# Four-layer decoder trunk on one core: VectorE's work on a finished set dealt out over the next set's steps, the last set's columns ended in two halves

## The chip, the cores and the metric

The kernel runs on one core of a Trainium2 chip. The metric is the device time of one execution in microseconds (us), the median of the runs shown. Engines are named as the profile names them: PE (TensorE, matmuls), PEld (its weight loads), DVE (VectorE), ACT (ScalarE), POOL (GpSimd) and SP (SyncE, which here issues the weight transfers).

## What is computed

The reference runs a trunk of depth 2 over 256 positions of width 2048, in float32. Layer 0 mixes with a recurrent head group and a pooling mixer, layer 1 with sparse attention. Each layer then runs an MLP and a gated embedding add, and a final norm closes:

```
hn = rmsnorm(h, ln_mix_g[i]);  h = h + mixer(hn)                       # w_in, w_out
hn = rmsnorm(h, ln_mlp_g[i]);  h = h + square(relu(hn @ w_up)) @ w_down   # 2048 -> 8192 -> 2048
gate = sigmoid(rmsnorm(h, ln_ple_g[i]) @ ple_w_gate[i])                # 2048 -> 2048
h = h + gate * (p[i] @ ple_w_proj[i])                                  # 256 -> 2048
return rmsnorm(h, ln_final_g)
```

## The kernel before, in words

**Products in three terms.** Every float32 weight is split as it arrives: ScalarE copies it to a rounded high part (`emit_hi`, L203), VectorE subtracts that from the weight and so makes the low part (`emit_lo`, L210). Activations are split in the same way. A product is three matmuls: high by high, low by high, high by low (`product`, L703 to L705). Only the third needs VectorE's low part.

**Steps and lookahead.** A list `steps` holds one entry for each half of a 1 MB weight load (two blocks of 128 rows by 512 columns). `run` goes through it: it emits the high parts up to two steps ahead, the step's matmuls (12 in a plain step), then what `after(n, fn)` put off to this step, and last the low part of the step two ahead. There are four buffers each for high and low parts, and three for raw loads. Each engine executes its own instructions strictly in the order in which they are emitted, so this order is the schedule.

**Sets.** The projections of 2048 output columns are done in two sets of 1024 columns (`mm_set`, index `n2`). A set accumulates over its steps into four PSUM banks, two 128-row halves of the positions (t) by two 512-column halves (n); the next set uses the other four. Two of the eight weight loads of an MLP set go through extra sums that save matmuls ("own" steps, `SUM_PAIRS`); their results come out in two side tiles `w`, made by `out1` to `out3` near the end of the set.

**The end of a set.** When the last matmul of a set is emitted, `post` puts the set's remaining work on the list. For a set of the MLP's down projection (`h_out`, 16 of them) VectorE does `wide` twice (L809, 1024 columns: the side tiles into h) and `adds` twice (L816, two instructions of 512 columns each: the banks into h); all of it is emitted with the set's last step, ahead of the low part of the step two later. Only the last two down sets of a layer (q = 3) also call `x_after`, which transposes the new h on TensorE (L787), splits it into the next input X, and squares it for the norm. The output projections of the mixers use the same `h_out`, without side tiles. The sets of the gate (`gate`, four of them) run a tanh on ScalarE (L998) and two VectorE instructions per 512-column piece (L1003, L1004), eight in all, again with the set's last step. In layer 1 the squares of the final norm (L1028) follow, and after the last set `finish` makes the reciprocal root, scales h in four pieces of 1024 columns (L1036) and sends them out (L1037). The small projection `proj` of the embedding is put between steps of each gate set.

Of the kernel before, what the change touches and what calls it, by code (L numbers as in the profile page):

```python
# [9 lines left out]
F32 = mybir.dt.float32  # L10
# [102 lines left out]
def trunk(ctx: ExitStack, tc: tile.TileContext, a: dict, out: bass.AP):  # L113
# [81 lines left out]
    def emit_hi(s):  # L195
        u, k0, nk = halves[s]["at"]
        dmas(u + AHEAD - 1)
        w = loads[u]["w"]
        if "add" not in halves[s]:
            halves[s]["src"] = loads[u]["raw"][:, k0:k0 + nk, :w]  # L200
        halves[s]["hi"] = hip.tile([P, 2, 512], F32R, name="hi")
        for k in (slice(0, 1), slice(1, nk)) if s == 0 else (slice(0, nk),):
            act.activation(halves[s]["hi"][:, k, :w], halves[s]["src"][:, k, :], AF.Copy)  # L203
# [33 lines left out]
    def after(n, fn):  # L237

        later.setdefault(state["step"] + n, []).append(fn)
# [440 lines left out]
    def wtiles():  # L680
        return utile().rearrange("p a b -> p (a b)").rearrange("p (n c) -> p n c", c=512), ph["w2"]

    def mm_set(src, order, X, post, own=(), S=None, between={}, hooks={}):


        B, n_set = ph["B"], ph["sets"]
# [80 lines left out]
        def out3():  # L767
            w1, w2 = w["w"]
            dve.scalar_tensor_tensor(w2[:, 1], w2[:, 0], -1.0, w2[:, 1], op0=OP.mult, op1=OP.subtract)

        for i, p in enumerate(order):
            if i in between:
                between[i]()
            if i in hooks:
                add_hook(hooks[i])
            parts = own_fns(p) if p in own else [(0, 2, None, plain(p, 0)), (2, 2, None, plain(p, 1))]
            add_blocks(src(p), parts)
# [21 lines left out]
    def h_out(n2, r, X, gi, sx=None, w_first=True):  # L799

        def post(w, banks):
            hb = lambda t, n: h[:, t, n2 * 1024 + n * 512:n2 * 1024 + (n + 1) * 512]

            def wide(t):
                ht = h[:, t, n2 * 1024:(n2 + 1) * 1024].rearrange("p (n c) -> p n c", c=512)
                if r is None:
                    dve.tensor_tensor(ht, ht, w[t], op=OP.add)
                else:
                    dve.scalar_tensor_tensor(ht, w[t], r[:, t:t + 1], ht, op0=OP.mult, op1=OP.add)  # L809

            def adds(n):
                for t in range(2):
                    if r is None:
                        dve.tensor_tensor(hb(t, n), hb(t, n), banks[t][n], op=OP.add)
                    else:
                        dve.scalar_tensor_tensor(hb(t, n), banks[t][n], r[:, t:t + 1], hb(t, n), op0=OP.mult, op1=OP.add)  # L816
            if w is not None:
                after(0, lambda: (wide(0), wide(1)))
            after(0, lambda: adds(0))
            after(0, lambda: adds(1))  # L820
            if X is not None:
                x_after(n2, banks, X, gi, sx)
        return post

    def x_after(n2, banks, X, gi, sx=None, at=0):
# [74 lines left out]
    def mlp(l, X, Xn):  # L900
# [3 lines left out]
        def up_out(q, n2):  # L904
            def post(w, banks):
                W = w or wtiles()

                def adds(n):
                    for t in range(2):
                        if w:  # L910
                            dve.tensor_tensor(W[t][:, n], banks[t][n], W[t][:, n], op=OP.add)  # L911

                def relu(n):
                    for t in range(2):
                        act.activation(W[t][:, n], W[t][:, n] if w else banks[t][n], AF.Relu)  # L915
                    for t in range(2):
                        act.activation(W[t][:, n], W[t][:, n], AF.Square)

                def back(n):
                    for i in (2 * n, 2 * n + 1):  # L920
                        turn(banks, i, lambda t, n, c: W[t][:, n, c * P:(c + 1) * P])

                def high(i):
                    k = 2 * i
                    act.activation(Hs[n2][:, k:k + 2, :T], scratch(banks, i), AF.Copy)  # L925

                def low(i):
                    k = 2 * i
                    dve.tensor_tensor(Hs[n2][:, k:k + 2, T:], scratch(banks, i), Hs[n2][:, k:k + 2, :T].bitcast(F32),  # L929
                                      op=OP.subtract)  # L930

                def sums():
                    v = [W[t][:, 1].rearrange("p (i j c) -> p i j c", j=2, c=P) for t in range(2)]
                    s_sums(v[0][:, :, 0], v[0][:, :, 1], v[1][:, :, 0], v[1][:, :, 1])

                def s_back(i):
                    b = scratch(banks, i).rearrange("p j (s n) -> p (j s) n", n=P)
                    for o in range(4):
                        pe.transpose(b[:, o], ph["f"][:, i, o], ident)

                def s_split(i):
                    b = scratch(banks, i).rearrange("p j (s n) -> p (j s) n", n=P)
                    S = ph["S"][1][:, i]
                    act.activation(S[:, :, :P], b, AF.Copy)
                    dve.tensor_tensor(S[:, :, P:], b, S[:, :, :P].bitcast(F32), op=OP.subtract)
                for n in range(2):
                    after(n, lambda n=n: (adds(n), relu(n)))
                    after(1 + n, lambda n=n: back(n))
                    for i in (2 * n, 2 * n + 1):
                        after(2 + n, lambda i=i: high(i))  # L950
                        after(2 + n, lambda i=i: low(i))
                if n2 == 0:
                    after(3, sums)
                    for i in range(2):
                        after(4, lambda i=i: s_back(i))
                        after(5, lambda i=i: s_split(i))
            return post

        Hs = []
# [16 lines left out]
    def ple(l, X, Xn):  # L976
# [11 lines left out]
            ph["sets"] = n_set  # L988

        def gate(n2):  # L990
            def post(w, banks):
                W = wtiles()
                at = 0
                hb = lambda t, n: h[:, t, n2 * 1024 + n * 512:n2 * 1024 + (n + 1) * 512]

                def tanh(n):
                    for t in range(2):
                        act.activation(W[t][:, n], banks[t][n], AF.Tanh, scale=HALF[:, t:t + 1])  # L998

                def add(n):  # L1000
                    for t in range(2):
                        e = st["e"][:, t, n2 * 1024 + n * 512:n2 * 1024 + (n + 1) * 512]
                        dve.scalar_tensor_tensor(W[t][:, n], W[t][:, n], 1.0, e, op0=OP.add, op1=OP.mult)  # L1003
                        dve.tensor_tensor(hb(t, n), hb(t, n), W[t][:, n], op=OP.add)  # L1004
                for n in range(2):
                    after(at, lambda n=n: tanh(n))
                    after(at, lambda n=n: add(n))
                if l == 0:
                    x_after(n2, banks, Xn, G_MIX + 16, at=at)
                    if n2 == 1:  # L1010
                        after(at + 4, rstd_of)
                else:
                    for n in range(2):
                        after(at, lambda n=n: last_squares(n2, n))
                    if n2 == 1:
                        after(at, finish)
            return post

        def load_e():
            st["e"] = big(F32, (P, 2, D))  # L1020
            if l == 1:
                st["g"] = big(F32, (P, 2, D))[:, 0]
                g = a["gfin"]
                nc.scalar.dma_start(st["g"], g.to_broadcast([P, D]))

        def last_squares(n2, n):
            for t in range(2):
                act.activation(jk, h[:, t, n2 * 1024 + n * 512:n2 * 1024 + (n + 1) * 512], AF.Square,  # L1028
                               accum_out=ssq[:, t, 2 * n2 + n:2 * n2 + n + 1])

        def finish():
            rstd_of()
            for t in range(2):
                for n2 in range(2):
                    c = slice(n2 * 1024, (n2 + 1) * 1024)
                    dve.scalar_tensor_tensor(h[:, t, c], h[:, t, c], RSTD[:, t:t + 1], st["g"][:, c], op0=OP.mult, op1=OP.mult)  # L1036
                    (nc.sync if n2 == 0 else nc.scalar).dma_start(out[:, t, c], h[:, t, c])  # L1037

        add_hook(load_e)
        for n2 in range(2):  # L1040
            mm_set(lambda p, n2=n2: a["ple_w_gate"][l][n2][p], range(8), X, gate(n2), between={5: lambda n2=n2: proj(n2)},
                   hooks={5: rstd_of} if n2 == 0 else {})
        add_hook(ph["close"])

    X1 = new_x()
# [340 lines left out]
```

## Time and profile before

| | us |
|---|---|
| median of 3 runs | 2342.57 (2340.16 to 2343.86) |
| the profiled execution, its own time | 2343.47 |
| its span, first to last instruction | 2341.4 |
| TensorE busy | 2283.6 (98%) |
| VectorE busy | 1738.2 (74%) |
| ScalarE busy | 1314.3 (56%) |
| mean granted TensorE clock | 0.995 |

How to read it: TensorE is busy nearly all of the span, and its matmuls overlap in the pipeline, so one of 512 columns is listed with 390 ns though the next starts 227 ns behind it. What can be won without changing the matmuls lies in the places where TensorE waits, in stretches at a lower clock, and behind the last matmul. The list of waits gives the first, the windows the second, the timeline the third.

### The profile page before, as it was taken

To read this page: it belongs to the slowest core of one execution; us is meant where nothing else is said; L and a number is where in the kernel's file an instruction comes from. 1 tells how busy PE (TensorE), PEld (TensorE's weight loads), DVE (VectorE), ACT (ScalarE), POOL (GpSimd) and SP (SyncE) were. 2 spreads that over 40 slices of the span, in tenths; PEclk is the share of its full clock that TensorE was granted. 3 is DMA by queue.
4 is the path that set the end of the run, shared out by engine and by line. 5 is a ranking of instruction groups with operands and counts; after the bars stand their busy time and mean duration, and the time that the engine had idled before them with its cause. 6 is when DMAs were issued, how large, how long until landed. Compare 5 with 4: busy or idle time off the path is not lost.

```text
span 2341.4 us, 30197 instructions
## 1 busy us (share of the span) xinstructions
PE 2283.6 (98%) x11510; PEld 1933.2 (83%) x11510; DVE 1738.2 (74%) x2360; ACT 1314.3 (56%) x1900; POOL 15.5 (1%) x42
## 2 busy tenths in 40 slices
PE   8999999999999999999999999999999999999997
PEld 8998887787787788888889988888788788788876
DVE  6786687788787788756875675688777877877864
ACT  6665564564465466555564554656456456455563
POOL 2000000000000000000000000000000000000000
PEclk9999999999999999999999999999999999999998
DMA  7545555555555555555775224555555555455553
GB/s 264 199 168 193 183 180 201 194 181 198 183 184 192 184 191 180 198 182 191 258 273 181 82 84 160 185 197 187 184 199 185 176 203 196 164 208 190 194 182 123
DMA packets 69264, 436.55 MB, mean 186 GB/s; under 512 B 9856, under 2 KB 14336, under 8 KB 18176
## 3 DMA queue, kind: packets, MB, share of 16 engines
q1 hardware_dynamic: 64272, 426.85, 52.2%
q10 hardware_dynamic: 4848, 7.79, 1.0%
q8 instruction: 90, 1.47, 0.3%
q14 instruction: 54, 0.44, 0.1%
HBM read 432.51 MB, written 2.10 MB: 186 GB/s over the span
## 4 chain that ended last, share of the span: by engine, by line
PE 94%; DVE 4%; issue 1%; DMA 1%; ACT 0%; SPq 0%; DVEq 0%; ACTq 0%
PE ps L705 24%; PE ps L703 24%; PE ps L704 24%; PE ps L293 10%; PE ps L297 3%; PE ps L787 2%; DVE lo L210 2%; PE ps L298 1%; PE ps L1328 1%; PE ps L1118 1%; DVE h L816 1%; DMA raw<-in_ab_w_in 1%; PE ps L1270 0%; PE ps L1268 0%; DVE h L1004 0%
## 5 line engine op out<-in xcount | busy, mean ns | idle before, releaser
L210 DVE TENSOR_TENSOR lo<-raw,hi 128x1024 fp32r<-128x1024 f32 (+1 forms) x817 | 937.9, 1166 | 228.8 <-ACT hi L203 227.2
L203 ACT ACTIVATE hi<-raw 128x1024 fp32r<-128x1024 f32 (+1 forms) x817 | 818.4, 1014 | 504.3 <-PE ps L704 396.1
L705 PE MATMUL ps<-lo,big 128*128 128x512 f32 x2496 | 976.3, 391 | 31.3 <-DVE lo L210 31.3
L703 PE MATMUL ps<-hi,big 128*128 128x512 f32 x2496 | 979.7, 393 | 0.0
L704 PE MATMUL ps<-hi,big 128*128 128x512 f32 x2496 | 973.7, 390 | 0.0
L705 PEld LDWEIGHTS ps<-lo,big 128*128 128x128 f32 x2496 | 469.9, 188 | 136.7 <-DVE lo L210 38.9
L704 PEld LDWEIGHTS ps<-hi,big 128*128 128x128 f32 x2496 | 470.4, 188 | 96.0
L703 PEld LDWEIGHTS ps<-hi,big 128*128 128x128 f32 x2496 | 470.2, 188 | 95.4
L293 PE MATMUL ps<-big,hi 128*128 128x256 f32 x1408 | 264.0, 289 | 7.2 <-ACT hi L203 7.2
L210 DVE TENSOR_TENSOR lo<-big,hi 128x1024 fp32r<-128x1024 f32 x128 | 156.6, 1223 | 136.8 <-ACT hi L203 136.8
L203 ACT ACTIVATE hi<-big 128x1024 fp32r<-128x1024 f32 x128 | 135.8, 1061 | 215.6 <-PE ps L704 201.7
L293 PEld LDWEIGHTS ps<-big,hi 128*128 128x128 f32 x1408 | 222.7, 193 | 9.2 <-ACT hi L203 7.2
L293 PE MATMUL ps<-big,lo 128*128 128x256 f32 x704 | 200.4, 285 | 2.5 <-DVE lo L210 2.5
L293 PEld LDWEIGHTS ps<-big,lo 128*128 128x128 f32 x704 | 135.6, 193 | 3.3 <-DVE lo L210 3.3
L297 PE MATMUL ps<-big,hi 128*128 128x512 f32 x320 | 113.6, 398 | 0.0
L298 PE MATMUL ps<-big,lo 128*128 128x256 f32 x320 | 89.7, 280 | 0.7 <-DVE lo L210 0.5
L734 DVE TENSOR_TENSOR big<-raw 128x1024 f32<-128x1024 f32 x64 | 78.0, 1219 | 0.2
L297 PEld LDWEIGHTS ps<-big,hi 128*128 128x128 f32 x320 | 60.1, 188 | 14.1
L929 DVE TENSOR_TENSOR big<-ps,big 128x512 fp32r<-128x512 f32 x64 | 41.1, 684 | 36.5 <-ACT big L925 36.5
L298 PEld LDWEIGHTS ps<-big,lo 128*128 128x128 f32 x320 | 60.3, 189 | 2.0 <-DVE lo L210 1.5
L409 ACT ACTIVATE big<-ps,gains 128x256 fp32r<-128x256 f32 x80 | 31.3, 474 | 49.5 <-PE ps L787 49.5
L915 ACT ACTIVATE u<-u 128x512 f32<-128x512 f32 x32 | 19.9, 623 | 55.5 <-DVE u L911 55.5
(235 smaller groups left out, 1525.2 us busy)
## 6 DMA issues: line engine op xcount, KB each, us to landing
raw<-in_mlp_w_up SPq DMA_DIRECT2D x128, 1024.0 KB, 4.9
raw<-in_mlp_w_down SPq DMA_DIRECT2D x128, 1024.0 KB, 4.9
raw<-in_c_w_in SPq DMA_DIRECT2D x36, 1024.0 KB, 4.9
raw<-in_ple_w_gate SPq DMA_DIRECT2D x32, 1024.0 KB, 4.9
raw<-in_ab_w_in SPq DMA_DIRECT2D x20, 1024.0 KB, 5.0
raw<-in_ab_w_out SPq DMA_DIRECT2D x16, 1024.0 KB, 4.9
raw<-in_c_w_out SPq DMA_DIRECT2D x16, 1024.0 KB, 4.9
raw<-in_c_cmp_w_k SPq DMA_DIRECT2D x8, 1024.0 KB, 4.9
```

Source lines behind the costliest of these rows:

```text
L203: act.activation(halves[s]["hi"][:, k, :w], halves[s]["src"][:, k, :], AF.Copy)
L210: dve.tensor_tensor(lo[:, k, :w], src[:, k, :], halves[s]["hi"][:, k, :w].bitcast(F32), op=OP.subtract)
L293: pe.matmul(b, lhsT=wt[:, kk, cols], rhs=x[:, x0:x0 + T], start=first and n == 0 and j % 2 == 0, stop=last and n == 2, skip_group_check=True)
L297: pe.matmul(b, lhsT=hi[:, kk, cols], rhs=x, start=first, stop=False, skip_group_check=True)
L298: pe.matmul(b[:, T:], lhsT=lo[:, kk, cols], rhs=x[:, :T], start=False, stop=last, skip_group_check=True)
L409: act.activation(dst[:, :T], src, AF.Copy, **kw)
L703: pe.matmul(b, lhsT=x_hi, rhs=hi[:, n, :], start=r not in begun, stop=False, skip_group_check=True)
L704: pe.matmul(b, lhsT=x_lo, rhs=hi[:, n, :], start=False, stop=False, skip_group_check=True)
L705: pe.matmul(b, lhsT=x_hi, rhs=lo[:, n, :], start=False, stop=end, skip_group_check=True)
L734: dve.tensor_tensor(t, raw[:, 0::3, :], raw[:, 1:2, :].to_broadcast([P, 2, 512]), op=OP.add)
L787: pe.transpose(b[:, j, t * P:(t + 1) * P], of(t, i // 2, (2 * i + j) % 4), ident)
L929: dve.tensor_tensor(Hs[n2][:, k:k + 2, T:], scratch(banks, i), Hs[n2][:, k:k + 2, :T].bitcast(F32), op=OP.subtract)
```

## The change

Four things are changed.

1. `h_out`: with side tiles, `wide(0)`, `wide(1)`, `adds(0)` and `adds(1)` are emitted one, two, three and four steps after the set's last step, each between two low parts; `x_after` moves with them by three steps. Without side tiles, `adds(1)` moves one step.
2. The gate's pieces: the second 512-column piece is emitted one step after the first. `proj` is put before the fifth weight load instead of the sixth. In `up_out` the sums of the side input move one step.
3. The final norm of layer 1: h times the gain vector is made piece by piece on VectorE (`hg`, two instructions per piece) for all pieces but the very last; the scale by the reciprocal root is then one factor per row.
4. The last set: the last two weight loads are used column half by column half (`column`), so that the banks of n = 0 end two steps before those of n = 1, and `last(0)` runs beside them. After the last tanh a one-element Sqrt (`warm`) brings ScalarE's function table in; `finish` scales the prepared pieces on ScalarE and VectorE and sends five pieces from SP.

```diff
@@ emit_hi
-            halves[s]["src"] = loads[u]["raw"][:, k0:k0 + nk, :w]
+            at = k0 if isinstance(k0, slice) else slice(k0, k0 + nk)
+            halves[s]["src"] = loads[u]["raw"][:, at, :w]
@@ mm_set
+        def column(p, n):
+            def fn(hi, lo):
+                for k in range(2):
+                    for t in range(2):
+                        product(PLAIN[t][n], A(p, k, t), hi, lo, k, k == 1 and p == order[-1])
+                if p == order[-1]:
+                    by_n(n, [acc_of(PLAIN[t][n]) for t in range(2)])
+            return fn
+
         for i, p in enumerate(order):
+            if by_n and i == len(order) - 2:
+                us = [len(loads), len(loads) + 1]
+                for q in order[i:]:
+                    loads.append({"src": src(q), "nk": 4, "w": 512})
+                for n in range(2):
+                    for u, q in zip(us, order[i:]):
+                        halves.append({"at": (u, slice(n, 4, 2), 2)})
+                        steps.append(("w", len(halves) - 1, column(q, n)))
+                return
@@ h_out
-            if w is not None:
-                after(0, lambda: (wide(0), wide(1)))
-            after(0, lambda: adds(0))
-            after(0, lambda: adds(1))
+            at = 0 if w is None else 3
+            for t in range(0 if w is None else 2):
+                after(1 + t, lambda t=t: wide(t))
+            for n in range(2):
+                after(at + n, lambda n=n: adds(n))
             if X is not None:
-                x_after(n2, banks, X, gi, sx)
+                x_after(n2, banks, X, gi, sx, at)
@@ up_out
-                    after(3, sums)
+                    after(4, sums)
...
@@ gate
+            def last(n, banks):
+                W = st.setdefault("W", None) or wtiles()
+                st["W"] = W if n == 0 else None
+                end = n2 == 1 and n == 1
+                for t in range(2):
+                    act.activation(W[t][:, n], banks[t], AF.Tanh, scale=HALF[:, t:t + 1])
+                if end:
+                    act.activation(warm, epsb, AF.Sqrt)
+                for t in range(2):
+                    dve.scalar_tensor_tensor(W[t][:, n], W[t][:, n], 1.0, eb(t, n), op0=OP.add, op1=OP.mult)
+                    dve.tensor_tensor(hb(t, n), hb(t, n), W[t][:, n], op=OP.add)
+                    last_square(t, n2, n)
+                for t in range(0 if end else 2):
+                    dve.tensor_tensor(hg(t, n), hb(t, n), gb(n), op=OP.mult)
+                if end:
+                    finish()
+
             def post(w, banks):
+                if l == 1:
+                    for n in range(2):
+                        after(n, lambda n=n: last(n, [banks[t][n] for t in range(2)]))
+                    return
...
                 for n in range(2):
-                    after(at, lambda n=n: tanh(n))
-                    after(at, lambda n=n: add(n))
+                    after(n, lambda n=n: tanh(n))
+                    after(n, lambda n=n: add(n))
...
         def finish():
-            rstd_of()
-            for t in range(2):
-                for n2 in range(2):
-                    c = slice(n2 * 1024, (n2 + 1) * 1024)
-                    dve.scalar_tensor_tensor(h[:, t, c], h[:, t, c], RSTD[:, t:t + 1], st["g"][:, c], op0=OP.mult, op1=OP.mult)
-                    (nc.sync if n2 == 0 else nc.scalar).dma_start(out[:, t, c], h[:, t, c])
+            mean_square()
+            act.activation(RSTD, MS, AF.Sqrt, scale=1.0 / D, bias=epsb)
+            dve.reciprocal(RSTD, RSTD)
+            o = st["hg"]
+            c = slice(1536, 2048)
+            for t in range(2):
+                r = RSTD[:, t:t + 1]
+                dve.scalar_tensor_tensor(o[:, t, c], h[:, t, c], r, st["g"][:, c], op0=OP.mult, op1=OP.mult)
+                b = slice(768 * t, 768 * t + 768)
+                act.activation(o[:, 0, b], o[:, 0, b], AF.Copy, scale=RSTD[:, 0:1])
+                nc.sync.dma_start(out[:, 0, b], o[:, 0, b])
+            nc.sync.dma_start(out[:, :, c], o[:, :, c])
+            for t in range(2):
+                b = slice(768 * t, 768 * t + 768)
+                dve.tensor_scalar(o[:, 1, b], o[:, 1, b], RSTD[:, 1:2], None, op0=OP.mult)
+                nc.sync.dma_start(out[:, 1, b], o[:, 1, b])
@@ the gate's sets
-            mm_set(lambda p, n2=n2: a["ple_w_gate"][l][n2][p], range(8), X, gate(n2), between={5: lambda n2=n2: proj(n2)},
-                   hooks={5: rstd_of} if n2 == 0 else {})
+            post, last = gate(n2)
+            mm_set(lambda p, n2=n2: a["ple_w_gate"][l][n2][p], range(8), X, post, between={4: lambda n2=n2: proj(n2)},
+                   hooks={5: rstd_of} if n2 == 0 else {}, by_n=last if l == 1 and n2 == 1 else None)
```

## Rows read from the trace of the kernel before

**Rows 1.** The page: busy us, share of the span, instructions.
```profile
PE 2283.6 (98%) x11510; PEld 1933.2 (83%) x11510; DVE 1738.2 (74%) x2360; ACT 1314.3 (56%) x1900; POOL 15.5 (1%) x42
```
**Rows 2.** Waits of PE, whole span: waiter, releaser, us in total, times, longest.
```profile
PE ps L705 <- DVE lo L210: 31.3, 18, 2.1
```
**Rows 3.** Timeline of PE, end of a down set: start, us, instruction, idle before.
```profile
434.23 0.39 PE L704 MATMUL ps<-hi,big 128*128 128x512 f32 x1
436.61 0.50 PE L705 MATMUL ps<-lo,big 128*128 128x512 f32 x1 [1.99 <-DVE lo L210]
436.95 0.40 PE L703 MATMUL ps<-hi,big 128*128 128x512 f32 x1
```
**Rows 4.** Timeline of DVE, the same stretch.
```profile
428.57 1.22 DVE L210 TENSOR_TENSOR lo<-raw,hi 128x1024 fp32r<-128x1024 f32 x1
...
430.31 1.28 DVE L809 SCALAR_TENSOR_TENSOR h<-u,rs,h 128x1024 f32<-128x1024 f32 x1
...
432.70 2.72 DVE L816 SCALAR_TENSOR_TENSOR h<-ps,rs,h 128x512 f32<-128x512 f32 x4
435.34 4.62 DVE L210 TENSOR_TENSOR lo<-raw,hi 128x1024 fp32r<-128x1024 f32 x4
```
**Rows 5.** Windows: stretch, us, busy time and instructions by engine, PEclk, DMA share, GB/s.
```profile
390.70:394.10 3.40, 3.40 (x9) 2.66 (x10) 3.20 (x3) 0.00 (x0) 0.00 (x0) 0.50 0.75 239
...
436.80:440.20 3.40, 3.40 (x16) 2.75 (x16) 3.25 (x4) 1.07 (x1) 0.00 (x0) 1.00 0.76 258
```
**Rows 6.** Timeline, one high and low part in an even stretch.
```profile
2284.94 1.06 ACT L203 ACTIVATE hi<-raw 128x1024 fp32r<-128x1024 f32 x1 [1.66 <-PE ps L704]
...
2286.03 1.23 DVE L210 TENSOR_TENSOR lo<-raw,hi 128x1024 fp32r<-128x1024 f32 x1 [1.50 <-ACT hi L203]
```
**Rows 7.** Waits of PE, 925 to 973 us: layer 0's last two down sets.
```profile
PE ps L705 <- DVE lo L210: 2.0, 2, 1.0
```
**Rows 8.** Waits of PE, 1023 to 1078 us: layer 0's two gate sets.
```profile
PE ps L293 <- DVE lo L210: 1.3, 1, 1.3
PE ps L705 <- DVE lo L210: 1.2, 1, 1.2
```
**Rows 9.** Timeline of DVE, end of layer 0's first gate set.
```profile
1018.12 0.69 DVE L1003 SCALAR_TENSOR_TENSOR u<-u,big 128x512 f32<-128x512 f32 x1 [4.75 <-ACT u L998]
...
1020.79 0.69 DVE L1003 SCALAR_TENSOR_TENSOR u<-u,big 128x512 f32<-128x512 f32 x1
...
1023.45 2.35 DVE L210 TENSOR_TENSOR lo<-raw,hi 128x1024 fp32r<-128x1024 f32 x2
```
**Rows 10.** The chain of waits, there: start, us, what.
```profile
1022.13 0.88 PE ps L787 x8
```
**Rows 11.** Timeline, end of layer 1's first gate set.
```profile
2271.71 0.69 DVE L1003 SCALAR_TENSOR_TENSOR u<-u,big 128x512 f32<-128x512 f32 x1 [4.75 <-ACT u L998]
...
2277.03 1.22 DVE L210 TENSOR_TENSOR lo<-raw,hi 128x1024 fp32r<-128x1024 f32 x1
...
2278.30 0.79 PE L705 MATMUL ps<-lo,big 128*128 128x512 f32 x1 [2.14 <-DVE lo L210]
```
**Rows 12.** Timeline, the end: last matmul; ScalarE, VectorE and SP after it.
```profile
2324.09 0.69 ACT L998 ACTIVATE u<-ps,rs 128x512 f32<-128x512 f32 x1 [8.01 <-PE ps L705]
...
2325.71 0.39 PE L705 MATMUL ps<-lo,big 128*128 128x512 f32 x1
...
2330.31 0.63 ACT L1028 ACTIVATE jk<-h 128x512 f32<-128x512 f32 x1 [0.61 <-DVE h L1004]
...
2331.05 1.28 ACT L384 ACT_TABLE_LOAD   x1
2332.35 0.30 ACT L384 ACTIVATE rs<-rs,epsb 128x2 f32<-128x2 f32 x1
...
2334.26 2.73 SPq L1037 DMA_DIRECT2D out<-h  x2
```
**Rows 13.** Windows, the output transfers.
```profile
2334.90:2340.30 5.40, 0.00 (x0) 0.00 (x0) 2.92 (x3) 0.00 (x0) 0.00 (x0) 0.50 0.95 388
```

More of the change, by code (lines that the diff above doesn't have):

```diff
@@ L681, in wtiles, with mm_set @@
         return utile().rearrange("p a b -> p (a b)").rearrange("p (n c) -> p n c", c=512), ph["w2"]
-    def mm_set(src, order, X, post, own=(), S=None, between={}, hooks={}):
+    def mm_set(src, order, X, post, own=(), S=None, between={}, hooks={}, by_n=None):
         B, n_set = ph["B"], ph["sets"]
@@ L952, in post @@
                 if n2 == 0:
-                    after(3, sums)
+                    after(4, sums)
                     for i in range(2):
-                        after(4, lambda i=i: s_back(i))
-                        after(5, lambda i=i: s_split(i))
+                        after(5, lambda i=i: s_back(i))
+                        after(6, lambda i=i: s_split(i))
             return post
@@ L990, in gate @@
         def gate(n2):
+            hb = lambda t, n: h[:, t, n2 * 1024 + n * 512:n2 * 1024 + (n + 1) * 512]
+            eb = lambda t, n: st["e"][:, t, n2 * 1024 + n * 512:n2 * 1024 + (n + 1) * 512]
+            gb = lambda n: st["g"][:, n2 * 1024 + n * 512:n2 * 1024 + (n + 1) * 512]
+            hg = lambda t, n: st["hg"][:, t, n2 * 1024 + n * 512:n2 * 1024 + (n + 1) * 512]
+            def last(n, banks):
[14 more added lines that the diff above has]
+                    finish()
             def post(w, banks):
+                if l == 1:
+                    for n in range(2):
+                        after(n, lambda n=n: last(n, [banks[t][n] for t in range(2)]))
+                    return
                 W = wtiles()
-                at = 0
-                hb = lambda t, n: h[:, t, n2 * 1024 + n * 512:n2 * 1024 + (n + 1) * 512]
                 def tanh(n):
@@ L1001, in add @@
                     for t in range(2):
-                        e = st["e"][:, t, n2 * 1024 + n * 512:n2 * 1024 + (n + 1) * 512]
-                        dve.scalar_tensor_tensor(W[t][:, n], W[t][:, n], 1.0, e, op0=OP.add, op1=OP.mult)
+                        dve.scalar_tensor_tensor(W[t][:, n], W[t][:, n], 1.0, eb(t, n), op0=OP.add, op1=OP.mult)
                         dve.tensor_tensor(hb(t, n), hb(t, n), W[t][:, n], op=OP.add)
                 for n in range(2):
-                    after(at, lambda n=n: tanh(n))
-                    after(at, lambda n=n: add(n))
[L1008 to L1017, printed above, removed]
+                    after(n, lambda n=n: tanh(n))
+                    after(n, lambda n=n: add(n))
+                x_after(n2, banks, Xn, G_MIX + 16)
+                if n2 == 1:
+                    after(4, rstd_of)
+            return post, last
         def load_e():
@@ L1022, in load_e, with last_square @@
                 st["g"] = big(F32, (P, 2, D))[:, 0]
+                st["hg"] = big(F32, (P, 2, D))
                 g = a["gfin"]
                 nc.scalar.dma_start(st["g"], g.to_broadcast([P, D]))
-        def last_squares(n2, n):
-            for t in range(2):
-                act.activation(jk, h[:, t, n2 * 1024 + n * 512:n2 * 1024 + (n + 1) * 512], AF.Square,
-                               accum_out=ssq[:, t, 2 * n2 + n:2 * n2 + n + 1])
-        def finish():
-            rstd_of()
+        def last_square(t, n2, n):
+            act.activation(jk, h[:, t, n2 * 1024 + n * 512:n2 * 1024 + (n + 1) * 512], AF.Square,
+                           accum_out=ssq[:, t, 2 * n2 + n:2 * n2 + n + 1])
@@ new lines, in finish @@
+        def finish():
+            mean_square()
[3 more added lines that the diff above has]
+            c = slice(1536, 2048)
+            for t in range(2):
+                r = RSTD[:, t:t + 1]
[4 more added lines that the diff above has]
+            nc.sync.dma_start(out[:, :, c], o[:, :, c])
```

## The prediction, made before the changed kernel ran

> **What bounds the kernel now.** I read the page first. TensorE is busy for 98% of the span, VectorE for 74% [rows 1], so matmuls that stay the same can give back only what TensorE loses between them. The list of its waits then names one loser: the third matmul of a product (L705) waits for VectorE's low part 18 times, 31.3 us in all, never over 2.1 us [rows 2]. The timelines of twelve of these places, the down sets of q = 0 to 2 in both layers, look alike, and one of them is shown. On VectorE the low part of the step two ahead stands behind two `wide` of 1.2 us each and four `adds` of 0.68 us, and comes at 435.34 instead of 430.3 [rows 4]. On TensorE the waiting matmul starts 2.38 us after its neighbour, the next 0.34 us later, where 0.227 is usual [rows 3]: a loss of 2.15 + 0.11 = 2.26 us. VectorE isn't short of time there (it is 74% busy): its order is wrong.
>
> A second loss shows in the windows. Behind some of these waits the granted clock is 0.50, which is 1.2 GHz, for 3.4 us: 9 matmuls start where 16 do at 1.00 [rows 5], so 7 x 0.227 = 1.6 us are lost. There are four such stretches in the span (from 390.7, 749.1, 1646.8 and 2278.3), each behind a wait of 2 us; nine other waits of 2 us have none, and no wait of 1.3 us or less has one.
>
> **The change part by part.**
>
> *Down sets, q = 0 to 2 (12 places).* `wide` and `adds` aren't removed, they are put behind low parts. VectorE reached the first `wide` at 430.31 [rows 4]; the low part takes that place, ends at 431.5, and TensorE wants it at 434.23 + 0.23 = 434.46 [rows 3]: 2.9 us early. In each of the next four steps VectorE has one low part (1.15 us by their spacing, 4.62 us for four) and one `wide` (1.2) or two `adds` (1.36) [rows 4], 2.4 to 2.5 us, against 12 x 0.227 = 2.72 us of matmuls. It doesn't fall back, and the 2.9 us stay as a reserve. High parts don't hold it up: in an even stretch a low part ends 2.3 us after its high part starts [rows 6], the start waits for the buffer of the step four before, and the part is used three steps (8.2 us) after that release. Nobody waits for h: the up sets read an older X, and the banks are wanted again in the next set's ninth step. So nothing takes the place of the wait. Gain 12 x 2.26 = 27.1 us, and 3 x 1.6 = 4.8 us of clock. Bounds: none of it, if the low parts stay late, to all of it; I take all, since each term has its own row.
>
> *Down sets of q = 3 (4 places).* The wait is 1.0 us, because TensorE's transposes stand in front of it [rows 7]; layer 1 shows the same 2.0 us for two. The split of X moves three steps; its four VectorE instructions beside a low part come to about 2.8 us in two of the steps (1.66 us for the four, by the timeline of the next set), which the reserve covers. X is wanted in the gate's ninth step. Gain 4 x (0.99 + 0.27) = 5.0 us.
>
> *Layer 0's gate sets (2).* Eight instructions run from 1018.12 to 1023.45, 0.67 us each, with the low part behind them [rows 9]. With four ahead of it, it starts at 1020.8 and ends at 1022.0; TensorE begins its transposes at 1022.13 and has 0.9 us of them before it wants it [rows 10]. The second four end at 1024.7 and the next low part at 1025.9, with that step's matmuls at 1026.6. Gain 1.25 + 1.33 [rows 8] + 2 x 0.27 = 3.1 us.
>
> *Layer 1's first gate set.* Here the work grows: four multiplications by the gain (`hg`) are added, so that each piece has six VectorE instructions, 4.0 us, and two such pieces stand ahead of two successive low parts; there are no transposes to cover them. From 2271.71 [rows 11]: six instructions to 2275.65, low part to 2276.85. TensorE wanted it at 2278.30 - 2.27 = 2276.03, so it loses 0.8. The second piece begins at 2277.0 (its tanh stands behind two squares and a high part on ScalarE), ends at 2280.9, low part at 2282.1; TensorE, running again from 2276.9, wants that at 2279.6: 2.5 us. With 0.11 each, 3.5 us against 2.14 + 0.27 + 1.6 of clock = 4.0 before. Gain 0.5 if the clock holds, a loss of 1.1 if it falls again.
>
> *The last set.* The column order leaves matmuls and bytes as they were. n = 0 now ends two steps before the end, and its six VectorE instructions stand ahead of the low part of the very last step. Let Y be the start of the last matmul of the n = 0 column. In [rows 12] the first tanh starts 0.42 us after the start of the last matmul of its bank, and VectorE follows 0.7 us later; here that bank's matmul is three before Y, so VectorE starts at Y + 0.4, the six end at Y + 4.3, the low part at Y + 5.5. TensorE wants it at Y + (1 + 12 + 2) x 0.227 = Y + 3.4. It loses 2.15 + 0.11 = 2.26 us, a wait that the kernel before doesn't have. Behind the last matmul (start X) the path gets shorter. Before: squares end and the table load starts at X + 5.3, root at X + 6.6, first output transfer at X + 8.55, end of the span at X + 15.7 [rows 12]. After: VectorE's four instructions run from X + 0.4 to X + 3.1, last square to X + 4.1, root at X + 4.4 (the table load lies beside VectorE's work), reciprocal and a ScalarE copy of 768 columns (0.85 us, between 0.69 for 512 and 1.06 for 1024 [rows 6, 12]): first transfer at X + 5.9. From there the transfers set the end: the 16 DMA engines are 0.95 busy until 2340.3 [rows 13], and from first issue to end took 7.1 us; smaller rows are allowed 0.1. End at X + 13.1, a gain of 2.6. Net gain 0.3, or a loss of 1.3 if the clock falls behind the new wait. Bounds of this part: +2.6 without the wait, -2 with a clock that falls for all that is left.
>
> The row shows a table load of 1.28 us with the root right behind it [rows 12]. The Trainium skill (ScalarE: Activation LUTs, What ACT_TABLE_LOAD costs) puts a drain of about 1.38 us more on each switch, 2.66 in all; by that the squares of the last piece would start 1.1 us later and so would the end. I go by the row.
>
> *At nothing:* the first `adds` of the mixers' output sets (no wait there before), `proj` one load earlier, and the sums of the up sets one step later: all of them lie beside matmuls with at least a step to spare; without that cover each is under 1.4 us once.
>
> **The sum.** 27.1 + 4.8 + 5.0 + 3.1 = 40.0, plus 0.5 and 0.3 for the two late places, 40.8; of these two waits of over 2 us I let one pull the clock down, which costs 1.6: 39.2. The profiled execution took 2343.47 (2.1 around the span), 0.9 above the median of 2342.57. I subtract from the median: 2303.4, rounded to 2303.5.
>
> **The rivals.**
>
> *Half the waits stay.* The order of the spread work is read from the code; if the reserve at the end of a set is smaller than 2.9 us, as it may be behind the short own steps, TensorE would wait about 1 us at each of the 16 down sets, as it does now where something covers part [rows 7]: 16 x 1.2 = 19 us of the gain gone, 2322. Against it: VectorE takes less than a step's time per step.
>
> *The wait only moves.* The pieces are the same, so the low parts are late by the same total, just spread over four steps: no change, about 2342. Against it: VectorE's 26% of idle time lies right behind these places, where it does four low parts in a row [rows 4].
>
> *Slower.* VectorE falls behind over the four steps after every set end. A reserve of 2.9 us and 4 x 2.72 of matmuls make 13.8 us; TensorE loses more than today's 2.26 us when low part and piece together take over 4.0 us a step instead of 2.5, say because reading banks while TensorE fills others slows VectorE. At 4.3 us a step each of 16 sets would lose 3.4 us, 2360. Against it: the four `adds` that read banks beside TensorE's matmuls already take 0.68 us each [rows 4].
>
> **How the numbers follow.** Forecast 0.82, half the waits 0.12, only moved 0.03, slower 0.03. Less than 0.2% (4.7 us) is what a measurement of this kernel can hardly tell from no change. Faster 0.95, same 0.03, slower 0.02 (a part of the slow case is small). The forecast's own range is 2299 to 2309: both late places without a loss and with the tail's full 2.6, to both with the clock down and 3 us of small waits beside them; it reaches to 2313 for part of the second case.
>
> **What would show it.** Right: PE's waits for L210 fall from 18 to two or three, at the end of layer 1's first gate set (0.8 and 2.5 us) and before the last step (2.1 us); three stretches at 0.50 are gone; `wide` and `adds` each stand between two low parts; the span ends 13 us after the last matmul starts. Wrong: waits of about 1 us after down sets, or low parts that wait for high parts there, or a last step without a wait.

## The result

The changed kernel takes 2303.22 us (median of 4 runs, 2302.09 to 2306.73) against 2341.36 us before (4 runs, 2338.43 to 2343.86). The ratio is 0.984, with a 95% interval of 0.9823 to 0.9857: 33 to 41 us less. The forecast was 2303.5.

The profiled execution is the slowest of the four, 2306.73 us with a span of 2304.7. Lines have moved: L706 is the third matmul (L705 before), L211 the low part, L829 and L836 are `wide` and `adds`, L1027 and L1028 the gate's two VectorE instructions in layer 1, L1031 the new `hg`. On the page, TensorE's share has risen, and the third matmul's waits for the low part have gone from 31.3 us to 4.8 (first line: busy us and share by engine; second line: busy us and mean ns of the group, then the idle time before it and its releaser). This answers to [rows 1, 2]:

```profile
PE 2277.0 (99%) x11510; PEld 1933.8 (84%) x11510; DVE 1734.8 (75%) x2365; ACT 1315.6 (57%) x1903; POOL 14.5 (1%) x42
...
L706 PE MATMUL ps<-lo,big 128*128 128x512 f32 x2496 | 973.2, 390 | 4.8 <-DVE lo L211 4.8
```

The list of TensorE's waits (total, times, longest) has three waits of the third matmul left:

```profile
PE ps L706 <- DVE lo L211: 4.8, 3, 2.1
```

VectorE's timeline after the down set that [rows 4] shows is the whole change in one view (start, us, instruction). The low part that stood behind 5 us of pieces now stands ahead of the first, and each piece lies between two low parts. TensorE has no wait here:

```profile
427.11 0.68 DVE L770 SCALAR_TENSOR_TENSOR big<-big 128x512 f32<-128x512 f32 x1
427.72 1.21 DVE L211 TENSOR_TENSOR lo<-raw,hi 128x1024 fp32r<-128x1024 f32 x1
428.85 1.27 DVE L829 SCALAR_TENSOR_TENSOR h<-u,rs,h 128x1024 f32<-128x1024 f32 x1
430.05 1.22 DVE L211 TENSOR_TENSOR lo<-raw,hi 128x1024 fp32r<-128x1024 f32 x1
431.18 1.28 DVE L829 SCALAR_TENSOR_TENSOR h<-big,rs,h 128x1024 f32<-128x1024 f32 x1
432.38 1.22 DVE L211 TENSOR_TENSOR lo<-raw,hi 128x1024 fp32r<-128x1024 f32 x1
433.51 1.40 DVE L836 SCALAR_TENSOR_TENSOR h<-ps,rs,h 128x512 f32<-128x512 f32 x2
434.83 1.21 DVE L211 TENSOR_TENSOR lo<-raw,hi 128x1024 fp32r<-128x1024 f32 x1
435.97 1.40 DVE L836 SCALAR_TENSOR_TENSOR h<-ps,rs,h 128x512 f32<-128x512 f32 x2
```

The three waits are where they were forecast: two at the end of layer 1's first gate set, one before the very last step. TensorE's timeline has them:

```profile
2237.02 0.50 PE L706 MATMUL ps<-lo,big 128*128 128x512 f32 x1 [0.69 <-DVE lo L211]
...
2242.15 0.50 PE L706 MATMUL ps<-lo,big 128*128 128x512 f32 x1 [2.07 <-DVE lo L211]
...
2287.05 0.50 PE L706 MATMUL ps<-lo,big 128*128 128x512 f32 x1 [2.05 <-DVE lo L211]
```

VectorE's timeline at the first of them shows why: six instructions (four of the piece, two `hg` listed as x2) stand ahead of each low part.

```profile
2231.88 0.69 DVE L1027 SCALAR_TENSOR_TENSOR u<-u,big 128x512 f32<-128x512 f32 x1 [4.75 <-ACT u L1023]
2232.61 0.69 DVE L1028 TENSOR_TENSOR h<-h,u 128x512 f32<-128x512 f32 x1
...
2234.55 1.28 DVE L1031 TENSOR_TENSOR big<-h,big 128x512 f32<-128x512 f32 x2
2235.75 1.22 DVE L211 TENSOR_TENSOR lo<-raw,hi 128x1024 fp32r<-128x1024 f32 x1
2237.00 0.69 DVE L1027 SCALAR_TENSOR_TENSOR u<-u,big 128x512 f32<-128x512 f32 x1
...
2239.67 1.29 DVE L1031 TENSOR_TENSOR big<-h,big 128x512 f32<-128x512 f32 x2
2240.88 2.35 DVE L211 TENSOR_TENSOR lo<-raw,hi 128x1024 fp32r<-128x1024 f32 x2
```

Behind both waits of 2 us the windows show the lower clock (columns as in [rows 5]): 9 matmuls in 3.3 us at 0.50.

```profile
2243.20:2246.50 3.30, 3.30 (x9) 2.65 (x8) 2.30 (x3) 1.14 (x2) 0.00 (x0) 0.50 0.63 206
2287.60:2290.90 3.30, 3.30 (x9) 2.30 (x7) 0.12 (x1) 0.69 (x1) 0.00 (x0) 0.50 0.00 0
```

This execution has a third such stretch near its start, ahead of all the work that the change moves. In the windows below, the first is of the changed kernel, the second of the kernel before. The stretch costs 15 x 0.11 = 1.7 us and is part of why this run is 3.5 us above the median of the four. Between it and the gate set the trace's clock record has no other, so the three behind down sets are gone.

```profile
6.50:21.50 15.00, 13.52 (x75) 12.49 (x76) 7.94 (x12) 9.37 (x15) 0.00 (x0) 0.89 0.97 349
```
```profile
6.50:20.50 14.00, 12.13 (x78) 11.51 (x79) 8.65 (x13) 10.09 (x17) 0.00 (x0) 1.00 1.00 373
```

It begins at 17.6 us, 0.6 us behind a wait of 1.15 us on TensorE's timeline. That no wait of 1.3 us or less has a stretch behind it, as the prediction saw, holds for the trace of the kernel before and not for this one:

```profile
17.00 0.39 PE L294 MATMUL ps<-big,lo 128*128 128x256 f32 x1 [1.15 <-DVE lo L211]
```

At the end, the last matmul starts at X = 2290.68. The timelines of TensorE, VectorE, ScalarE and SP answer to [rows 12]. The table load lies beside VectorE's work, the root comes at X + 4.35 instead of X + 6.64, the first output transfer at X + 5.84 instead of X + 8.55, and the span ends at X + 14.0 instead of X + 15.7. The load isn't hidden in full here: VectorE's last h is ready at 2293.53, and its square starts 0.55 us later, behind the load and the square before it. In the run with layer 1's first gate set later, whose last matmuls are at the full clock, it is 0.1 us (2286.56, then 2286.65).

```profile
2290.68 0.52 PE L706 MATMUL ps<-lo,big 128*128 128x512 f32 x1
```
```profile
2292.84 0.69 DVE L1028 TENSOR_TENSOR h<-h,big 128x512 f32<-128x512 f32 x1
```
```profile
2291.94 1.28 ACT L1025 ACT_TABLE_LOAD   x1
2293.23 0.20 ACT L1025 ACTIVATE warm<-epsb 128x1 f32<-128x1 f32 x1
...
2294.08 0.63 ACT L1067 ACTIVATE jk<-h 128x512 f32<-128x512 f32 x1
...
2295.03 0.30 ACT L1072 ACTIVATE rs<-rs,epsb 128x2 f32<-128x2 f32 x1 [0.23 <-DVE rs L376]
```
```profile
2296.52 1.17 SPq L1081 DMA_DIRECT2D out<-big  x2
2297.74 0.62 SPq L1082 DMA_DIRECT2D out<-big  x1
2298.41 1.79 SPq L1086 DMA_DIRECT2D out<-big  x2
```

### The profile page after: what moved, and what is told of

Same layout as the page of the kernel before. It is cut to its first block, busy times and chain, and to the rows that moved or that the text cites. A ratio compares the mean times of both kernels' runs of the same rounds, so it can differ in the third digit from the quotient of the medians.

```text
span 2304.7 us, 30201 instructions
## 1 busy us (share of the span) xinstructions
PE 2277.0 (99%) x11510; PEld 1933.8 (84%) x11510; DVE 1734.8 (75%) x2365; ACT 1315.6 (57%) x1903; POOL 14.5 (1%) x42
## 4 chain that ended last, share of the span: by engine, by line
PE 97%; DVE 1%; ACT 1%; DMA 0%; issue 0%; SPq 0%; DVEq 0%; ACTq 0%
PE ps L706 25%; PE ps L704 25%; PE ps L705 25%; PE ps L294 11%; PE ps L298 3%; PE ps L807 2%; PE ps L299 1%; PE ps L1378 1%; PE ps L1168 1%; DVE lo L211 0%; DMA raw<-in_ab_w_in 0%; PE ps L1320 0%; PE ps L1318 0%; PE ps L960 0%; PE ps L587 0%; PE ps L1321 0%
## 5 line engine op out<-in xcount | busy, mean ns | idle before, releaser
L211 DVE TENSOR_TENSOR lo<-raw,hi 128x1024 fp32r<-128x1024 f32 (+1 forms) x817 | 941.2, 1165 | 193.9 <-ACT hi L204 193.4
L706 PE MATMUL ps<-lo,big 128*128 128x512 f32 x2496 | 973.2, 390 | 4.8 <-DVE lo L211 4.8
L705 PE MATMUL ps<-hi,big 128*128 128x512 f32 x2496 | 973.0, 390 | 0.0
L706 PEld LDWEIGHTS ps<-lo,big 128*128 128x128 f32 x2496 | 469.4, 188 | 103.9 <-DVE lo L211 6.1
L705 PEld LDWEIGHTS ps<-hi,big 128*128 128x128 f32 x2496 | 469.5, 188 | 95.6
L211 DVE TENSOR_TENSOR lo<-big,hi 128x1024 fp32r<-128x1024 f32 x128 | 156.5, 1223 | 120.2 <-ACT hi L204 120.2
L866 DVE SCALAR_TENSOR_TENSOR big<-ps,gains,big 128x256 fp32r<-128x256 f32 x80 | 33.2, 476 | 25.1 <-ACT big L410 20.4
```

The costliest lines, as they stand in the source:

```text
L211: dve.tensor_tensor(lo[:, k, :w], src[:, k, :], halves[s]["hi"][:, k, :w].bitcast(F32), op=OP.subtract)
L705: pe.matmul(b, lhsT=x_lo, rhs=hi[:, n, :], start=False, stop=False, skip_group_check=True)
L706: pe.matmul(b, lhsT=x_hi, rhs=lo[:, n, :], start=False, stop=end, skip_group_check=True)
L866: dve.scalar_tensor_tensor(X(k)[:, T:], scratch(banks, i)[:, j], gain(k), X(k)[:, :T].bitcast(F32), op0=OP.mult, op1=OP.subtract)
```

## The experiments

All are the changed kernel with one edit, but two: "before, down sets alone" is the kernel before with one, and "both later" has two.

| kernel | median us | ratio to before | 95% interval |
|---|---|---|---|
| changed | 2303.22 | 0.9840 | 0.9823 to 0.9857 |
| down sets undone | 2338.72 | 0.9996 | 0.9986 to 1.0005 |
| all four pieces in one lump | 2311.49 | 0.9876 | 0.9861 to 0.9890 |
| before, down sets alone | 2303.95 | 0.9845 | 0.9830 to 0.9860 |
| last set in the usual order | 2304.41 | 0.9844 | 0.9830 to 0.9859 |
| last set's first piece later | 2301.31 | 0.9831 | 0.9818 to 0.9845 |
| layer 1's first gate set later | 2299.57 | 0.9824 | 0.9811 to 0.9837 |
| both later | 2296.08 | 0.9811 | 0.9797 to 0.9824 |
| two queues for the output | 2302.95 | 0.9841 | 0.9828 to 0.9855 |

The ratios are to runs of the kernel before from the same set: 2341.36 us beside the changed kernel, 2339.82 beside the first four experiments, 2340.01 beside the last four. A difference between two rows of other sets is uncertain by 1 to 2 us for that.

**Down sets undone.**

```diff
-            at = 0 if w is None else 3
-            for t in range(0 if w is None else 2):
-                after(1 + t, lambda t=t: wide(t))
-            for n in range(2):
-                after(at + n, lambda n=n: adds(n))
+            at = 0
+            if w is not None:
+                after(0, lambda: (wide(0), wide(1)))
+            after(0, lambda: adds(0))
+            after(0, lambda: adds(1))
```

> The changed kernel with the four pieces of h_out put back into the set's last step (16 down sets). If the sum of the prediction is right, the 12 waits of 2.0 us and the four of 1.0 us are back with about three stretches at half clock: 27.1 + 5.0 + 4.8 = 36.9 us more than the changed kernel, about 2340. Rival, the gain comes as much from the gates and the end as from the down sets: about 2322.

Measured: 2338.72, 35.5 us more than the changed kernel and not to be told from the kernel before. Its 19 waits are the 16 of the down sets and the three of the changed kernel; the list of TensorE's waits has

```profile
PE ps L706 <- DVE lo L211: 32.7, 19, 2.1
```

The rival with half the gain elsewhere falls.

**The down sets alone.** The part of `h_out` that the edit above takes out, put into the kernel before.

> The kernel before with the h_out part of the change alone. If the parts add up: 36.9 us less than the kernel before, about 2304.5, with the waits at the gate sets left (1.25, 1.33 and 2.1 us). Rival, the parts depend on each other (gates and proj take up the reserve): a gain of less than 30 us.

Measured: 2303.95, a gain of 35.9 us. The two ways of taking the part's worth, 35.5 and 35.9, agree, so it doesn't lean on the rest, and the rival (under 30) falls. The list of waits shows what it leaves, the gate sets of both layers (of the two waits of L293 the one of 0.3 us lies near the kernel's start):

```profile
PE ps L705 <- DVE lo L210: 3.4, 2, 2.1
PE ps L293 <- DVE lo L210: 1.6, 2, 1.3
```

**One lump.** Same pieces, same VectorE time, one step later, not dealt out; `x_after` moves by one step instead of three.

```diff
-            at = 0 if w is None else 3
-            for t in range(0 if w is None else 2):
-                after(1 + t, lambda t=t: wide(t))
-            for n in range(2):
-                after(at + n, lambda n=n: adds(n))
+            at = 0 if w is None else 1
+            if w is not None:
+                after(1, lambda: (wide(0), wide(1)))
+            for n in range(2):
+                after(at if w is not None else n, lambda n=n: adds(n))
```

> The changed kernel with all four pieces of h_out (5.2 us of VectorE) in one lump one step later, so behind the low part of the step two ahead and in front of the one after it. If order and the reserve of 2.9 us decide: the first low part is in time, the next ends about 0.7 us late at the 12 down sets with q below 3, none at q = 3 where transposes give 0.9 us; no clock loss: 12 x 0.9 = 11 us more than the changed kernel, about 2314. Rival, dealing out over four steps is what counts (a lump costs the same wherever it stands): waits of 2 us again, about 2340. Second rival, the reserve is larger than worked out: no waits, 2303.

Measured: 2311.49, 8.3 us more than the changed kernel. On VectorE one low part now stands ahead of the lump and the rest behind it, and TensorE waits 0.41 us at each of the 12 sets instead of 1.99 (VectorE's timeline, then TensorE's):

```profile
426.88 1.22 DVE L211 TENSOR_TENSOR lo<-raw,hi 128x1024 fp32r<-128x1024 f32 x1
428.01 1.28 DVE L829 SCALAR_TENSOR_TENSOR h<-u,rs,h 128x1024 f32<-128x1024 f32 x1
...
433.04 5.98 DVE L211 TENSOR_TENSOR lo<-raw,hi 128x1024 fp32r<-128x1024 f32 x5
```
```profile
434.32 0.50 PE L706 MATMUL ps<-lo,big 128*128 128x512 f32 x1 [0.41 <-DVE lo L211]
```

So most of the gain is one low part passing the pieces; dealing them out over four steps is worth the last 8 us. Both rivals fall: the lump costs neither the same wherever it stands (2340) nor nothing (2303). The expected wait of 0.7 us was too long.

**The last set in the usual order.**

```diff
-                   hooks={5: rstd_of} if n2 == 0 else {}, by_n=last if l == 1 and n2 == 1 else None)
+                   hooks={5: rstd_of} if n2 == 0 else {})
```

> The changed kernel with the last two loads in the usual order (both column halves of the last set end together; the two pieces and the finish follow). TensorE has no wait of 2 us and no half clock before its last step (2.3 + 1.3 to 1.6 us sooner done), but both pieces lie behind the last matmul: first output transfer about 8.3 us after it starts instead of 5.8, so 2.4 us later. Prediction's view: within 1.5 us of the changed kernel. Rival, the halved end is worth what it hides (some 4 us of VectorE work): 4 us more than the changed kernel.

Measured: 2304.41, 1.2 us more than the changed kernel, within the spread of the runs. As expected, only the two waits at the gate set are left, and the tail is longer: the last matmul starts at 2284.26, the first transfer at X + 8.6, and the span ends at X + 16.7 instead of X + 14.0.

```profile
2284.26 0.39 PE L706 MATMUL ps<-lo,big 128*128 128x512 f32 x1
```
```profile
2292.83 1.17 SPq L1081 DMA_DIRECT2D out<-big  x2
```

As the change stands, its two halves are worth next to nothing: of the 2.7 us that they take off the tail, 2.2 come back as the wait before the last step, and more where the clock falls behind it.

**The last set's first piece later.** Then the wait should be an order too.

```diff
                 if p == order[-1]:
-                    by_n(n, [acc_of(PLAIN[t][n]) for t in range(2)])
+                    banks = [acc_of(PLAIN[t][n]) for t in range(2)]
+                    if n == 0:
+                        after(1, lambda: by_n(0, banks))
+                    else:
+                        by_n(n, banks)
```

> The changed kernel with the n = 0 piece of the last set emitted one step later, so behind the low part of the very last step. Theory (an instruction order, not a shortage of VectorE): the wait of 2.05 us before the last step is gone, and with it the half clock behind it, while the tail behind the last matmul is as long: 2.3 to 3.8 us less than the changed kernel, about 2300. Rival, the piece then ends too late and the tail grows by what the wait shrinks: 2303.

Measured: 2301.31, 1.9 us less than the changed kernel, where 2.3 to 3.8 were expected; two waits are left of three (2.8 us), both at the gate set. The tail kept its length: the last matmul starts at 2285.86 and the span ends at 2299.8, X + 13.9. The difference of the medians alone couldn't carry this; with the list of waits it does. Against the last set in the usual order it is 3.1 us, and all five runs (2299.89 to 2301.80) lie below all four of that kernel (2303.06 to 2304.51): that is about what the halves are worth once they delay nothing.

**Layer 1's first gate set later.**

```diff
-                for t in range(0 if end else 2):
-                    dve.tensor_tensor(hg(t, n), hb(t, n), gb(n), op=OP.mult)
+                def gains_in():
+                    for t in range(2):
+                        dve.tensor_tensor(hg(t, n), hb(t, n), gb(n), op=OP.mult)
+                if n2 == 0:
+                    after(3 if n == 0 else 2, gains_in)
+                elif not end:
+                    gains_in()
...
-                        after(n, lambda n=n: last(n, [banks[t][n] for t in range(2)]))
+                        after(1 + 2 * n, lambda n=n: last(n, [banks[t][n] for t in range(2)]))
```

> The changed kernel with layer 1's first gate set dealt out further: its first piece one step later, its second three, the multiplications by the gain at steps four and five. Theory: the waits of 0.7 and 2.1 us there are gone: 3.0 us less, and 1.5 more where the clock fell behind them, so 2299 to 2300. Rival, ScalarE's order (tanh, squares, high parts) keeps the low parts late: a wait of 1 us or more stays.

Measured: 2299.57, 3.6 us less. One wait is left:

```profile
PE ps L706 <- DVE lo L211: 2.0, 1, 2.0
```

That wait had no stretch at half clock behind it this time: ten matmuls start in 2.3 us.

```profile
2281.20:2283.50 2.30, 2.30 (x10) 1.77 (x10) 0.00 (x0) 0.41 (x1) 0.00 (x0) 1.00 0.00 0
```

**Both later.**

> Both of these edits. If they are independent, no wait of VectorE's low parts is left behind the sets and no half clock but behind the last matmul: 5 to 8 us less than the changed kernel, 2296 to 2298.

Measured: 2296.08, 7.1 us less than the changed kernel and the fastest kernel here. The intervals of the two ratios to the kernel before overlap by a hair (0.9797 to 0.9824, 0.9823 to 0.9857), but all four runs (2295.75 to 2296.97) lie below every run of the changed kernel. L706 is gone from the list of TensorE's waits, which now reads, whole,

```profile
PE ps L294 <- ACT hi L204: 8.3, 1, 8.3
PE ps L1365 <- DVE big L1361: 0.5, 1, 0.5
PE ps L299 <- DVE lo L211: 0.5, 1, 0.5
PE ps L1366 <- DVE big L1361: 0.3, 1, 0.3
PE ps L294 <- DVE lo L211: 0.3, 1, 0.3
```

The 8.3 us are the wait for the first weights, where the kernel before has 7.2.

**Two queues for the output.** The third and fifth of the output transfers issued from ScalarE.

> The changed kernel with two of the five output transfers issued from ScalarE instead of SP. In the changed kernel SP's last issues take 0.6, 0.6 and 1.1 us instead of 0.35, and the end comes 8.2 us after the first issue where 7.2 was predicted. If the one queue costs that, the end comes 0.5 to 1 us sooner, 2302.5. Rival, the bytes set it (or the smaller rows): no change.

Measured: 2302.95, 0.3 us less, no difference. From the first issue (2292.27) to the end of the span (2300.2) it takes 7.9 us, in the changed kernel 8.2. So one queue instead of two explains at most 0.3 of the 1.0 us by which the end came later than forecast.

## Why the prediction was right

**The down sets.** 27.1 + 4.8 + 5.0 = 36.9 us were forecast; undoing them costs 35.5, doing them alone brings 35.9. The three terms can't be told apart by medians, since stretches at half clock come and go between executions. The term for the clock leaned on one execution, 2343.47 us, near the top of its kernel's runs, with three stretches behind down sets; the kernel with the down sets undone, profiled at 2339.98, has two behind the same 16 waits. The mechanism is shown by the waits: 16 gone, none new at these places, which answers the prediction's three rivals.

**Its grounds.** That VectorE's order and not its load was wrong is what the lump shows: with the same work in the same engine, one low part ahead of it takes the wait from 1.99 to 0.41 us. The reserve was judged 0.3 us too small.

**Layer 0's gate sets.** Both waits are gone from the changed kernel, as forecast. Their 3.1 us can't be seen by themselves: gates and end together were to bring 3.1 + 0.5 + 0.3 less 1.6 of clock, 2.3 us. With the down sets undone the rest is worth 1.1 us (interval -1.2 to 3.3, from 0.9986 to 1.0005 of 2340), and between the down sets alone and the whole change lie 0.7 us.

**The two late places.** Forecast were waits that put TensorE back by 0.8 and 2.5 us at the gate set and 2.15 before the last step; the profile has 0.69, 2.07 and 2.05 of idle time, which with the 0.16 that a waiting matmul loses beyond its idle time [rows 3] is 0.85, 2.23 and 2.21. The second was sized too long by 0.3: the second piece began 5.12 us behind the first (2231.88 to 2237.00), where 5.3 was worked out, and TensorE wanted the low part at 2242.15 - 2.23 = 2239.92, 8.04 us behind that start, where 7.9 was.

**The clock.** I let one of the two waits pull it down. In the profiled run both did. Over the profiled runs of the changed kernel and its variants, such a wait (2.0 to 2.1 us at these two places) had a stretch at 0.50 behind it in 5 of 11 cases: in the changed kernel at both places, with the lump and with the down sets undone at the last set alone, and with the last piece later at the gate set; not at the gate set in four others, nor at the last set with the gate set later or with two queues. (The four are the lump, the down sets undone, the usual order and two queues. Of the two kernels with the old gate set, the kernel before has a stretch there and the down sets alone have none.) One of two is thus a fair mean; what decides it in a single run stays open.

**The tail.** The first transfer came at X + 5.84, forecast X + 5.9. The step from there to the end was mis-sized: 8.2 us instead of 7.2, so the tail gained 1.7 us and not 2.6. The forecast allowed 0.1 for smaller rows. The windows give 0.4 to the transfers themselves, 5.7 us at 367 GB/s where the kernel before has 5.3 us at 396; they have rows of 3072 and 2048 bytes instead of 4096 per partition, but that these are the cause isn't shown:

```profile
2297.00:2302.70 5.70, 0.00 (x0) 0.00 (x0) 1.03 (x2) 0.32 (x1) 0.00 (x0) 0.50 0.94 367
```
```profile
2335.00:2340.30 5.30, 0.00 (x0) 0.00 (x0) 2.82 (x3) 0.00 (x0) 0.00 (x0) 0.50 0.97 396
```

The other 0.6 lies behind the last landing, where SP's closing waits and the drains of the engines stand: the trace has it at X + 12.54, and the end 1.45 us later, where the kernel before has X + 14.88 and 0.8. Why they take longer stays open; with two queues it is still 1.2 us.

**The table load.** The trace has the load for 1.28 us and the next instruction at 2293.23, 0.01 us behind it. The Trainium skill (ScalarE: Activation LUTs, What ACT_TABLE_LOAD costs) puts a drain of about 1.38 us on top of the load at each switch. No such drain shows here: the row decides, and the sum was right to go by it.

**The sum.** 39.2 us were forecast and 38.1 measured. The tail's 0.9 and the 0.3 of the second wait have opposite signs. That the time itself came within 0.3 us is luck: the gain was 1.1 us too small, and the kernel before measured 2341.36 beside the changed one, 1.2 below the 2342.57 that the forecast started from. The medians of one kernel differ by 1.5 us between sets of runs.

## What to carry to other kernels

When one engine feeds another through an in-order queue, look at what stands ahead of the part that is wanted next, not only at how busy the engine is: VectorE was 74% busy and still cost TensorE 31 us of waits, and moving one instruction ahead of 5 us of others won most of it back (27 of 35.5 us with the lump). Work that nobody waits for belongs behind the parts that the bottleneck wants next, and each new piece put ahead of such a part (here the multiplications by the gain, and the early half of the last set) must be worked out in the same way: at layer 1's first gate set the change made two waits out of one, and it made a new one before the last step. A column order that ends half the work early brings next to nothing as long as the early half stands ahead of the last step's operand; behind it, it brought 3.1 us.

## What the runs showed of the hardware

The same wait of 2.05 us of TensorE had a stretch of 3.4 us at half clock behind it in some runs and none in others, with the same instructions around it. This costs 1.6 us each time and is part of the spread of a kernel's runs: of the 13 runs of the kernel before beside the first experiments, the six with a mean granted clock of 0.997 took 2338.2 to 2338.9 us, the five with 0.995 took 2341.3 to 2343.5.

SP took about 0.6 us for the third and the fourth and 1.14 us for the fifth output transfer instead of 0.35, when all five were issued within 2.6 us. Issuing two of them from ScalarE brought the end at most 0.3 us closer to the first issue.
